# Four more inner tiles of the output weights by seven block products, and the tail woven from token halves

## The chip, the cores and the metric

The kernel runs on one core of a Trainium2 chip (trn2). A core has TensorE (PE, matmuls into PSUM, which has eight banks of 512 floats per partition), VectorE (DVE), ScalarE (ACT), GpSimd (POOL) and SyncE (SP). Each engine works off its own list of instructions in order and waits on semaphores for the others. DMAs are issued here from SP's and POOL's lists, and a few from ScalarE's. The metric is device time in microseconds, the median of several runs; lower is better.

## The reference

One decoder block on 512 tokens of width 1024: a SwiGLU feed-forward (FFN1), a token-mixing layer (pooling and dilated attention), a second SwiGLU (FFN2), each behind an RMSNorm that the conditioning vector scales and shifts, and a final RMSNorm.

```python
D_MODEL, SEQ, D_FF = 1024, 512, 2816
def swiglu(u, w_in, w_out):
    a, b = jnp.split(u @ w_in, 2, axis=-1)
    return (jax.nn.silu(a) * b) @ w_out

u = modulate(rmsnorm(h, g_norm_ffn1[l]), sh1, sc1)
h = h + 0.5 * gt1 * swiglu(u, w_ffn1_in[l], w_ffn1_out[l])
u = modulate(rmsnorm(h, g_norm_mix[l]), sh2, sc2)
h = h + gt2 * token_mixing(u, ...)
u = modulate(rmsnorm(h, g_norm_ffn2[l]), sh3, sc3)
h = h + 0.5 * gt3 * swiglu(u, w_ffn2_in[l], w_ffn2_out[l])
return rmsnorm(h, g_final)
```

The change is in the two products with w_out, [512 x 2816] by [2816 x 1024].

## The kernel before

**Layout and precision.** Activations lie transposed: a tile is 128 features by 512 tokens. The inner width 2816 is 22 inner tiles (`FT`), the output width 1024 is eight output tiles `H[0..7]` (`KT`), which hold the residual stream. Each float32 operand is split in a high and a low part of type fp32r, and a product is three matmuls: high by high, high by low, low by high (`mm3`, lines 358 to 360). ScalarE makes the high part of a weight chunk (`split_hi`, line 313), VectorE the low part (`split_lo`, line 327).

**Chunks.** `plan` lists in `order` all weight chunks in the order in which matmuls take them, and in `loads` the DMAs from HBM (512 KB a chunk of 1024 columns). Loads go to five buffers: three `raw` ones, and two parts of `X` in the FFNs. The split parts go into a ring of seven chunks (`RING`). `look(n)` issues loads into free buffers and splits chunks up to n ahead of the one that is taken next; `take` hands over the next one. `shift` and `shifted` only move where in the ring a chunk begins, by 16 columns.

**Seven products.** A product of two by two blocks needs eight block products; a scheme of sums and differences needs seven (Strassen's, in Winograd's form). For the weights, `blocks` lays a group of four loads out as seven chunks, of which four are differences that `make` computes on VectorE (line 252). A chunk listed in `outer` gets its low part in another way: ScalarE writes its negated high part (line 309) and POOL issues a DMA that adds the chunk from HBM (line 311). Token halves T1 and T2 (256 columns each) are the blocks of the other side. `duo` does two inner tiles of the first product of an FFN that way (lines 769 to 771), and `out_quad` four inner tiles of the second (lines 891 to 893), into three pairs of PSUM banks A, B, C, with partial sums copied to SBUF (`D`, line 873). `h_sums` makes the sums of the inner activations that it needs (lines 853 to 859), and `later` and `step` put such work a number of products later.

**Order of an FFN.** `ffn` goes through `PARTS` of the inner tiles. For each part it computes the inner tiles that are due (`ffn_pair` plain, or `duo`), and then that part's share of the output: plain matmuls for the first part of FFN1, `out_quad` for other parts, and for the last part, tiles 16 to 21, a **tail**: eight chunks of 768 columns, the first ones by 512 columns (lines 1053 to 1056), the last four or five output tiles by token halves (`out_tail` for FFN1, `out_end` for FFN2), a bank to each tile and half.

**End of an FFN.** For each tile VectorE updates H (`scalar_tensor_tensor`, line 515), ScalarE squares it (line 516), VectorE adds the squares up (`acc`). `stats_t` brings the sum over features by tiny matmuls (line 449), a square root on ScalarE and a reciprocal on VectorE (line 454); `spread` spreads the result over partitions by two matmuls (line 459). The first token half's statistics are taken while matmuls of the second half run. After FFN1 `norm_steps` computes the mixing stage's operands UH and UL from it (lines 466, 478, 492) and `head` begins that stage, with the splits of its first four chunks made ahead. After FFN2 `out_end` scales the tiles (line 567), multiplies by the spread reciprocal (line 571, VectorE and POOL) and stores them (line 574).

**Looking ahead.** Inside `out_quad` and later duos five chunks ahead are split; in the first duo of each FFN `look(3 + i // 3 if first else 5)`; `ffn_pair` three or four. The first `out_quad` is at 145 us (FFN1) and 722 us (FFN2) of the profile.

Of the kernel before, what the change touches and what calls it, by code (L numbers as in the profile page):

```python
# [14 lines left out]
P = 128  # L15
T = 512
# [39 lines left out]
def lay_ffn(w_in, w_out, first, plain, blocks):  # L56
# [16 lines left out]
    for k0, k1 in PARTS:  # L73
        if blocks <= k0 and k1 < FT:
            for i, c in ((0, 0), (0, 4), (1, 4), (1, 0)):
                rows = w_out[(k0 + 2 * i) * P:(k0 + 2 * i + 2) * P]
                quads.append(np.concatenate([_fmajor(rows, x) for x in _tiles(*((c + m) * P for m in range(4)))], axis=1))
            continue
        for m in range(KT):
            outs.append(_fmajor(w_out[k0 * P:k1 * P], np.arange(m * P, (m + 1) * P)))  # L80
    n = len(outs) - KT
    outs = [np.concatenate(outs[i:i + 2], axis=1) for i in range(0, n, 2)] + outs[n:]
    return ins, outs[:-KT] + quads + outs[-KT:]
# [43 lines left out]
PARTS = ((0, 4), (4, 8), (8, 12), (12, 16), (16, 22))  # L127
# [8 lines left out]
def chunk_widths():  # L136
    outs = [D] * (KT // 2 * (len(PARTS) - 1)) + [(FT - PARTS[-1][0]) * P] * KT
# [5 lines left out]
class Kernel:  # L143
# [6 lines left out]
    def plan(self):  # L150
# [12 lines left out]
        self.shifted, self.outer = set(), {}  # L163
# [8 lines left out]
        def blocks(recs, outer=0):  # L172
# [5 lines left out]
            self.shifted.update(range(len(self.order), len(self.order) + 7))  # L178
# [14 lines left out]
        def ffn(n, ins, outs, first):  # L193
# [4 lines left out]
            for part, (k0, k1) in enumerate(PARTS):  # L198
                while j < pairs_before(n, part):
# [8 lines left out]
                put = blocks if (n or part) and part < len(PARTS) - 1 else plain  # L208
                put(outs[part * KT // 2:(part + 1) * KT // 2] if part + 1 < len(PARTS) else outs[-KT:],
                    **({"outer": (3, 0, 2)[n]} if put is blocks else {}))  # L210

        ffn(0, f1i, f1o, FIRST)
        shift(3)
# [5 lines left out]
        shift(4)  # L219
# [298 lines left out]
    def out_tail(self, ms, ksrc, gate, nxt, squares):  # L518
# [5 lines left out]
        step = None  # L524
# [32 lines left out]
    def out_end(self, ms, ksrc, gate):  # L557
# [3 lines left out]
        tiles = {}  # L561
        A, Bh = slice(0, HT), slice(HT, T)
        rA, rB = self.B[6], self.B[7]
        self.held = self.pos

        def scaled(m, hs):
            nc.scalar.activation(self.O[m][:, hs], self.H[m][:, hs], AF.Copy, scale=self.g(3)[:, m:m + 1])

        def final(e, m, hs, r):
            o = self.O[m][:, hs]  # L570
            e.tensor_tensor(o, o, r[:, hs], op=OP.mult)

        def store(m0, m1, hs, queue):
            queue.dma_start(self.out[m0 * P:m1 * P, hs].rearrange("(m p) t -> p m t", p=P), self.OO[:, m0:m1, hs])

        for h, hs in enumerate((A, Bh)):
            for m in ms:
                bank = self.nb()
                if h == 0:
                    tiles[m] = ksrc(m)  # L580
                    self.split_hi()
                    if m == ms[0]:
                        nc.scalar.preload_act_table(AF.Sqrt)
                n = len(tiles[m])
                for i, (hi, lo, uh, ul) in enumerate(tiles[m]):
                    if h and m == ms[1] and i == n // 2:
                        self.stats_t(rA, A)
                    if h and m == ms[2] and i == n // 2:
                        self.spread(rA, A)
                        nc.scalar.activation(self.R[:, A], rA[:, A], AF.Copy)  # L590
                        for j in range(4):
                            final(g, j, A, self.R)
                            if j % 2:
                                store(j - 1, j + 1, A, nc.sync)
                    self.mm3(bank[:, hs], hi, lo, uh[:, hs], ul[:, hs], i == 0, i == n - 1)
                s = self.tp.tile([P, T], F32, name="ut")[:, :HT]
                self.tail_step(m, hs, bank, gate, s)
                if h and m == ms[-1]:
                    break
                scaled(m, hs)  # L600
                self.split_lo()
                v.tensor_tensor(self.acc[:, hs], self.acc[:, hs], s, op=OP.add)
                if h and m in ms[2:4]:
                    j = 4 + 2 * (m - ms[2])
                    for x in (j, j + 1):
                        final(v, x, A, rA)
                    store(j, j + 2, A, nc.sync)

# [7 lines left out]
        self.stats_t(rB, Bh, (self.acc[:, Bh], s))  # L616
        warm(2)
        scaled(ms[-1], Bh)
# [16 lines left out]
    def head(self, n, banks, table):  # L635
# [9 lines left out]
        for h, hs in enumerate((A, Bh)):  # L645
            for i, (k, which) in enumerate(steps if h == 0 else [(k, both) for k in range(KT)]):
                if h == 0:
                    stepA(min(i, 5) + 3)
                    if i == 4:
                        self.stats_t(self.B[7], Bh)  # L650
# [34 lines left out]
    def hpair(self, j):  # L685

        if self.nh == 4 and j == PARTS[-1][0] + 4:
            if not self.extra:
                self.extra = self.fw.tile([P, 2 * T], F32R, name="kept2"), self.Gall[:, :2 * T]
            return self.extra  # L690
# [19 lines left out]
    def ffn_pair(self, j, beside=lambda: None):  # L710
# [4 lines left out]
        pb = self.ffn_tile(ahead)  # L715
# [57 lines left out]
    def duo(self, j, first, last):  # L773
# [19 lines left out]
        HHp, HLp = (q(x) for x in self.hpair(j))  # L793
# [5 lines left out]
        def high():  # L799
            copy(HHp[:, :, ts, :], q(c)[:, :, ts, :])  # L800
# [927 lines left out]
```

## Time and profile before

| | us |
|---|---|
| median of 3 runs | 1002.2 (1002.18 to 1004.14) |
| the profiled execution, its own time | 1001.14 |
| its span, first to last instruction | 999.4 |
| TensorE busy | 984.8 |
| VectorE busy | 807.2 |
| ScalarE busy | 544.9 |
| tail of FFN1, first matmul to the mixing stage's first | 319.06 to 353.20 |
| tail of FFN2, first to last of its matmuls | 954.41 to 988.66 |

A row of the profile's groups names line, engine, operation, output and inputs with shapes and count, then busy time and the mean of one in ns, then idle time ahead of it and what ended it. Rows of the timeline begin with start and duration in us. A matmul's duration holds its way through the array, so matmuls overlap; from start to start they are closer than the duration says.

### The profile page before, as it was taken

To read this page: it belongs to the slowest core of one execution; us is meant where nothing else is said; L and a number is where in the kernel's file an instruction comes from. 1 tells how busy PE (TensorE), PEld (TensorE's weight loads), DVE (VectorE), ACT (ScalarE), POOL (GpSimd) and SP (SyncE) were. 2 spreads that over 40 slices of the span, in tenths; PEclk is the share of its full clock that TensorE was granted. 3 is DMA by queue.
4 is the path that set the end of the run, shared out by engine and by line. 5 is a ranking of instruction groups with operands and counts; after the bars stand their busy time and mean duration, and the time that the engine had idled before them with its cause. 6 is when DMAs were issued, how large, how long until landed. Compare 5 with 4: busy or idle time off the path is not lost.

```text
span 999.4 us, 17017 instructions
## 1 busy us (share of the span) xinstructions
PE 984.8 (99%) x6868; PEld 915.4 (92%) x6868; DVE 807.2 (81%) x1229; ACT 544.9 (55%) x824; POOL 67.0 (7%) x75
## 2 busy tenths in 40 slices
PE   8999999999999999999999999999999999999997
PEld 6888899999999999889988888898999999999996
DVE  6979979999996677879567777569798989989654
ACT  6453277786766443333414233465577868676652
POOL 0000001110110000007100000000010110010001
PEclk9999999999999999999999999999999999999999
DMA  9867567867857223123265774323376567567502
GB/s 338 278 212 251 190 169 211 222 184 216 241 126 198 89 78 106 57 92 125 77 235 185 266 267 133 96 73 106 111 169 192 143 171 179 156 151 204 137 17 85
DMA packets 49601, 163.29 MB, mean 163 GB/s; under 512 B 5617, under 2 KB 8945, under 8 KB 49522
## 3 DMA queue, kind: packets, MB, share of 16 engines
q1 hardware_dynamic: 42354, 137.95, 40.5%
q0 software_dynamic: 6480, 23.60, 14.2%
q8 instruction: 54, 0.88, 0.4%
q10 hardware_dynamic: 688, 0.66, 0.2%
q14 instruction: 25, 0.20, 0.1%
HBM read 159.41 MB, written 2.77 MB: 162 GB/s over the span
## 4 chain that ended last, share of the span: by engine, by line
PE 94%; DVE 3%; DMA 1%; ACT 1%; issue 1%; DVEq 0%; ACTq 0%; POOLq 0%
PE bank L358 13%; PE bank L359 13%; PE bank L360 13%; PE bank L771 10%; PE bank L769 10%; PE bank L770 10%; PE bank L891 4%; PE bank L893 4%; PE bank L892 4%; PE bank L1658 2%; PE bank L1662 1%; PE bank L1660 1%; PE bank L1249 1%; DMA wlo<-wf1o 1%; PE bank L1430 1%; PE bank L1431 1%
## 5 line engine op out<-in xcount | busy, mean ns | idle before, releaser
L327 DVE TENSOR_TENSOR wlo<-raw,whi 128x1024 fp32r<-128x1024 f32 (+5 forms) x129 | 140.3, 1099 | 45.3 <-ACT whi L313 45.1
L313 ACT ACTIVATE whi<-raw 128x1024 fp32r<-128x1024 f32 (+5 forms) x157 | 148.1, 955 | 18.9 <-DMA raw<-wmix 6.3
L358 PE MATMUL bank<-UH,whi 128*128 128x512 f32 (+1 forms) x432 | 158.1, 366 | 0.0
L359 PE MATMUL bank<-UL,whi 128*128 128x512 f32 (+1 forms) x432 | 154.0, 357 | 0.1
L360 PE MATMUL bank<-UH,wlo 128*128 128x512 f32 (+1 forms) x432 | 153.9, 356 | 0.0
L771 PE MATMUL bank<-UH,wlo 128*128 128x256 f32 x512 | 141.4, 276 | 0.0
L769 PE MATMUL bank<-UH,whi 128*128 128x256 f32 x512 | 141.4, 276 | 0.0
L770 PE MATMUL bank<-UL,whi 128*128 128x256 f32 x512 | 141.4, 276 | 0.0
L769 PE MATMUL bank<-SH,whi 128*128 128x256 f32 x384 | 107.0, 279 | 0.0
L771 PE MATMUL bank<-SH,wlo 128*128 128x256 f32 x384 | 106.9, 278 | 0.0
L770 PE MATMUL bank<-SL,whi 128*128 128x256 f32 x384 | 106.8, 278 | 0.0
L313 ACT ACTIVATE whi<-X 128x1024 fp32r<-128x1024 f32 (+3 forms) x109 | 90.5, 854 | 20.8 <-DVE X L252 20.7
L770 PEld LDWEIGHTS bank<-UL,whi 128*128 128x128 f32 x512 | 96.2, 188 | 0.1
L769 PEld LDWEIGHTS bank<-UH,whi 128*128 128x128 f32 x512 | 96.1, 188 | 0.1
L327 DVE TENSOR_TENSOR wlo<-X,whi 128x1024 fp32r<-128x1024 f32 (+3 forms) x92 | 83.1, 927 | 16.1 <-ACT whi L313 16.0
L771 PEld LDWEIGHTS bank<-UH,wlo 128*128 128x128 f32 x512 | 96.1, 188 | 0.0
L360 PEld LDWEIGHTS bank<-UH,wlo 128*128 128x128 f32 x432 | 81.1, 188 | 12.1
L359 PEld LDWEIGHTS bank<-UL,whi 128*128 128x128 f32 x432 | 81.2, 188 | 11.8 <-issue 0.5
L358 PEld LDWEIGHTS bank<-UH,whi 128*128 128x128 f32 x432 | 81.2, 188 | 11.3 <-issue 0.5
L770 PEld LDWEIGHTS bank<-SL,whi 128*128 128x128 f32 x384 | 72.5, 189 | 0.0
L769 PEld LDWEIGHTS bank<-SH,whi 128*128 128x128 f32 x384 | 72.5, 189 | 0.0
L771 PEld LDWEIGHTS bank<-SH,wlo 128*128 128x128 f32 x384 | 72.4, 189 | 0.0
(340 smaller groups left out, 2402.5 us busy)
## 6 DMA issues: line engine op xcount, KB each, us to landing
ada<-wada SPq DMA_DIRECT2D x47, 512.0 KB, 5.3
raw<-wmix SPq DMA_DIRECT2D x43, 512.0 KB, 4.1
raw<-wf1i SPq DMA_DIRECT2D x32, 512.0 KB, 6.2
raw<-wf2i SPq DMA_DIRECT2D x30, 512.0 KB, 4.5
AR<-wada SPq DMA_DIRECT2D x16, 512.0 KB, 4.1
wlo<-wf2i POOLq DMA_DIRECT2D x16, 512.0 KB, 5.7
X<-wf2i SPq DMA_DIRECT2D x14, 512.0 KB, 5.2
raw<-wf1o SPq DMA_DIRECT2D x12, 512.0 KB, 5.0
```

Source lines behind the costliest of these rows:

```text
L313: self.nc.scalar.activation(self.hi[:, y], r[:, x], AF.Copy)
L327: self.nc.vector.tensor_tensor(self.lo[:, y], r[:, x], self.hi[:, y], op=OP.subtract)
L358: M(ps, hi, uh, start=start, stop=False)
L359: M(ps, hi, ul, start=False, stop=False)
L360: M(ps, lo, uh, start=False, stop=stop)
L769: M(o, hi, uh, start=start and p == 0 and k == 0, stop=False, skip_group_check=True)
L770: M(o, hi, ul, start=False, stop=False, skip_group_check=True)
L771: M(o, lo, uh, start=False, stop=k == 3, skip_group_check=True)
L891: M(o, hi, uh, start=start and m % 2 == 0 and k == 0, stop=False, skip_group_check=True)
L892: M(o, hi, ul, start=False, stop=False, skip_group_check=True)
L893: M(o, lo, uh, start=False, stop=k == 1, skip_group_check=True)
L1658: M(b, hi, self.UH[k], start=k == 0, stop=False)
```

## The change

The output weights' last part is split in two: tiles 16 to 19 go through `out_quad` like the parts ahead, and tiles 20 and 21 go plain, by token halves, in the new `out_last`, which takes the place of the sixth step's rest, of the seventh product and of the old tails. In the plan, two plain chunks of 1024 columns (`rest`) stand ahead of the last chunk of that group of seven. `out_tail`'s place in FFN1 and the loops of `out_end` go; `out_end` keeps what comes after the last matmul. `duo` and the last plain tile look five chunks ahead throughout, and the last duo's high and low parts come by `later` in any case. In FFN1 tiles 20 and 21 get buffers of their own (HX, HY), and the steps of `trig` that stand beside duos begin one duo earlier.

```diff
-PARTS = ((0, 4), (4, 8), (8, 12), (12, 16), (16, 22))
+PARTS = ((0, 4), (4, 8), (8, 12), (12, 16), (16, 20), (20, 22))
...
-    outs = [D] * (KT // 2 * (len(PARTS) - 1)) + [(FT - PARTS[-1][0]) * P] * KT
+    outs = [D] * (KT // 2 * (len(PARTS) - 1) + 2)
...
-        def blocks(recs, outer=0):
+        def blocks(recs, outer=0, rest=()):
...
+                if rest and make == (x0, r21, x1):
+                    self.tail.append(len(self.order))
+                    plain(rest)
...
+                if n or part:
+                    blocks(recs, (3, 0, 2)[n], outs[-2:] if part + 2 == len(PARTS) else ())
...
-        pb = self.ffn_tile(ahead)
+        pb = self.ffn_tile(ahead + (j + 1 == PLAIN[0]))
...
-            self.look(3 + i // 3 if first else 5)
+            self.look(5)
...
-        if last:
-            mult()
-            high()
-            low()
-        else:
-            self.later(1, mult)
-            n = 8 if self.nh == 4 and j % 4 == 0 else 2
-            self.later(n, high)
-            self.later(n, low)
+        self.later(1, mult)
+        n = 8 if self.nh == 4 and j % 4 == 0 and j < PARTS[-1][0] else 2
+        self.later(n, high)
+        self.later(n, low)
...
-        self.ffn_post(3, self.ffn_silu(3, pa), self.ffn_tile(4), lambda low: self.later(1, low))
+        self.ffn_post(3, self.ffn_silu(3, pa), self.ffn_tile(5), lambda low: self.later(1, low))
...
+                if tail:
+                    return tail(A, B, C, D, lambda m, w: product(bank, u, start, (m,), w))
...
+    def out_last(self, n, gate, A, B, C, D, product):
+        self.held = self.pos
+        w = self.take() + self.take()
+        h = [self.hh(k) for k in range(*PARTS[-1])]
...
+        def plain(banks, m, t, start=False):
+            for k in range(2):
+                (hi, lo), (hh, hl) = w[2 * m + k], h[k]
+                o = half(banks, m)
+                M(o, hi, hh[:, t], start=start and m % 2 == 0 and k == 0, stop=False, skip_group_check=True)
+                M(o, hi, hl[:, t], start=False, stop=False, skip_group_check=True)
+                M(o, lo, hh[:, t], start=False, stop=k == 1, skip_group_check=True)
...
+        def two(m, t, acc, first):
+            o = acc if first else sq[:, m % 4 // 2 * T:m % 4 // 2 * T + T]
+            for i in range(2):
+                square(m + i, t, o[:, i * HT:(i + 1) * HT])
+            for i in range(2):
+                scaled(m + i, t)
+            if not first:
+                v.tensor_tensor(acc, acc, o, op=OP.add)
...
+        for m in range(4):
+            plain(C, m, T1)
+            to_h(m, half(C, m), T1)
+            if m % 2:
+                two(m - 1, T1, self.acc, m == 1)
+        for b in range(2):
+            more()
+            for i in range(2):
+                plain(B, 4 + 2 * b + i, T1)
+            v.tensor_tensor(D[b][:, :, 0, :], r(B[b]), D[b][:, :, 0, :], op=OP.add)
+            for i in range(2):
+                to_h(4 + 2 * b + i, D[b][:, i, 0, :], T1)
+            two(4 + 2 * b, T1, self.acc, False)
+            self.split_lo()
+        w6 = self.take()
+        for b in range(2):
+            more()
+            for i in range(2):
+                plain(C, 4 + 2 * b + i, T2, True)
+            v.tensor_tensor(D[b][:, :, 1, :], r(C[b]), D[b][:, :, 1, :], op=OP.add)
+            for i in range(2):
+                to_h(4 + 2 * b + i, D[b][:, i, 1, :], T2)
+            two(4 + 2 * b, T2, late, b == 0)
+            self.split_lo()
+        step = None
+        for m in range(4):
+            more()
+            if m == 1:
+                self.stats_t(rA, T1, (self.acc[:, :HT], self.acc[:, HT:]))
+            elif m == 2:
+                self.spread(rA, T1)
+                if n:
+                    self.final_first(rA)
+                else:
+                    step = self.norm_steps(1, T1)
+                    step(0)
+            product(m, w6)
+            plain(A, m, T2)
+            s = sq[:, m * HT:(m + 1) * HT]
+            to_h(m, half(A, m), T2)
+            square(m, T2, s)
+            if m < 3:
+                scaled(m, T2)
+            if step:
+                step(1 if m < 3 else 3)
+            self.split_lo()
+            x = late[:, m % 2 * HT:m % 2 * HT + HT]
+            if m < 3 or not n:
+                v.tensor_tensor(x, x, s, op=OP.add)
+            self.fetch()
+            if n and m == 2:
+                self.final_second(rA)
```

Here `half(banks, m)` is one half of a bank: tiles 0 and 1 share a bank, tiles 2 and 3 the next. `to_h` is the update of H on VectorE, `square` and `scaled` are ScalarE's, `more` makes the high part of the next weight chunk if the mixing stage's four are not yet split. `final_first` has POOL multiply and SP store four tiles of the first token half, `final_second` has VectorE do the other four.

More of the change, by code (lines that the diff above doesn't have):

```diff
@@ L559, in out_end, with final_second @@
+    def final_second(self, rA):
+        nc, A = self.nc, slice(0, HT)
+        for j in range(4, KT):
+            self.final(nc.vector, j, A, rA)
+            if j % 2:
+                self.store(j - 1, j + 1, A, nc.sync)
+    def out_end(self, gate, parts):
         nc = self.nc
         v, g = nc.vector, nc.gpsimd
[L561 to L607, printed above, removed]
@@ L771, in product, with duo @@
                 M(o, lo, uh, start=False, stop=k == 3, skip_group_check=True)
-    def duo(self, j, first, last):
+    def duo(self, j, first):
         nc, v = self.nc, self.nc.vector
@@ L883, in out_quad, with product @@
         p5 = [r(p5[:, i * T:(i + 1) * T]) for i in range(2)]
-        def product(banks, u, start):
-            w = self.take()
-            for m in range(4):
+        def product(banks, u, start, ms=range(4), w=None):
+            w = w or self.take()
+            for m in ms:
                 o = banks[m // 2][:, m % 2 * HT:m % 2 * HT + HT]
@@ L914, in out_quad @@
                     copy(D[b][:, :, 0, :], r(A[b]))
-                elif i == 3:
+                elif i == 3 and not tail:
                     for m in (2 * b, 2 * b + 1):
@@ L919, in out_quad @@
                     copy(D[b][:, :, 1, :], r(A[b]))
-                elif i == 5:
+                elif i == 5 and not tail:
                     v.tensor_tensor(D[b][:, :, 0, :], r(B[b]), D[b][:, :, 0, :], op=OP.add)
@@ L996, in ffn @@
                 else:
-                    if not tail and j == k1:
+                    if j == k1:
                         self.h_sums(k0, PLAIN[n])
-                    self.duo(j, last, tail and j + 2 == FT)
+                    self.duo(j, last)
                     last = None
@@ L1003, in ffn @@
                 last = self.beside_out(part) or last
+            if part + 2 == len(PARTS):
+                self.sums.close()
+                if n:
+                    op = self.f2.enter_context(self.tc.tile_pool(name="f2o", bufs=1))
+                    self.OO = op.tile([P, KT * T], F32, name="out").rearrange("p (m t) -> p m t", m=KT)
+                    self.O = [self.OO[:, m, :] for m in range(KT)]
+                else:
+                    self.sums = ExitStack()
+                    xp = self.sums.enter_context(self.tc.tile_pool(name="f1x", bufs=1))
+                    self.extra = [xp.tile([P, 2 * T], F32R, name=x) for x in ("HX", "HY")]
+                nc.scalar.preload_act_table(AF.Sqrt)
+                self.out_quad(k0, gate, lambda *x: self.out_last(n, gate, *x))
+                continue
```

167 lines of the change are left out of this document (83 added, 84 removed).

## The prediction

> **What bounds the kernel now.** I read the page first, then TensorE's waits, then the stretches of the two tails, then single rows.
>
> ```profile
> span 999.4 us, 17017 instructions
> ...
> PE 984.8 (99%) x6868; PEld 915.4 (92%) x6868; DVE 807.2 (81%) x1229; ACT 544.9 (55%) x824; POOL 67.0 (7%) x75
> ```
>
> TensorE is busy for all but 14.6 us, so time goes where matmuls go, or where TensorE is made to wait. The waits, largest first inside the two FFNs (engine and line, what it waited for, us, times, longest):
>
> ```profile
> PE bank L893 <- DMA wlo<-wf1o: 1.3, 1, 1.3
> PE bank L891 <- ACT bank L873: 1.2, 1, 1.2
> PE bank L891 <- ACT sl L794: 0.7, 1, 0.7
> ```
>
> Stretches (us, then busy time and instructions of PE, PEld, DVE, ACT, POOL, then clock and DMA). First an output block by seven products without a wait, then the first such block of each FFN; then the old tail of FFN1 in full-width and half-token matmuls, then that of FFN2:
>
> ```profile
> 782.09:801.13 19.04, 19.04 (x170) 19.04 (x169) 17.69 (x23) 16.02 (x22) 2.17 (x3) 1.00 0.68 172
> 145.16:165.78 20.62, 19.33 (x171) 19.13 (x169) 19.40 (x25) 16.70 (x24) 1.75 (x2) 1.00 0.70 167
> 722.11:743.69 21.58, 19.65 (x170) 19.25 (x169) 20.39 (x27) 17.02 (x25) 2.67 (x3) 1.00 0.65 154
> ...
> 319.06:335.40 16.34, 16.34 (x74) 13.52 (x73) 10.88 (x12) 8.71 (x12) 0.00 (x0) 1.00 0.56 159
> 335.40:353.20 17.80, 17.80 (x154) 17.79 (x152) 11.34 (x24) 6.89 (x14) 0.00 (x0) 1.00 0.28 85
> ...
> 954.41:966.68 12.27, 12.27 (x57) 10.14 (x55) 7.21 (x8) 6.36 (x9) 0.00 (x0) 1.00 0.00 1
> 966.68:988.66 21.98, 21.98 (x189) 21.98 (x188) 10.80 (x25) 10.53 (x23) 3.01 (x4) 1.00 0.06 19
> ```
>
> The reader is to see three things. A block of 168 matmuls of 256 columns takes 19.04 us, **0.1133 each**; 72 of 512 columns take 16.34, 0.227 each: time goes by columns. The first block of FFN1 takes 20.62 and that of FFN2 21.58, so 1.6 and 2.5 us of waiting stand there. And both tails run without a wait, with VectorE at 50 to 65%: they have slack on VectorE, and TensorE sets them.
>
> **The change: matmuls.** The old tail has 6 weight tiles x 8 output tiles x 3 matmuls of 512 columns, which is 288 halves. The new one has 7 products of 24 halves (168) and 2 tiles x 8 x 2 halves x 3 (96): 264. So 24 fewer per FFN, 2.7 us, 5.4 in all, if nothing waits.
>
> **Weights and queues.** Six loads of 512 KB replace eight of 384 KB per FFN, the same bytes, and two issues fewer on SP. Three low halves in FFN1 and two in FFN2 now come by an accumulating DMA on POOL's queue, re-reading 512 KB each, with a negating copy on ScalarE. Four block differences on VectorE, the sums of the activations and wider splits come too. I cost these at nothing up to the sixth product: the block at 782.09 carries the same work (DVE 17.69 of 19.04, ACT 16.02) and does not wait. With that cover gone each VectorE operation of 1024 would cost its 1.2 us. The last duo's high and low halves, once immediate, are late in no case, since the first products do not read tiles 20 and 21.
>
> **Five chunks ahead.** In the first duo a chunk is split one product (2.7 us) earlier. What that meets:
>
> ```profile
> 137.30 9.49 DMA wlo<-wf1o
> ...
> 146.84 0.38 PE bank L893
> ```
> ```profile
> 702.98 0.69 DVE L670 TENSOR_TENSOR X<-u,bank 128x512 f32<-128x512 f32 x1 [1.16 <-PE bank L360]
> 704.37 0.69 DVE L680 TENSOR_TENSOR HK<-X,HI 128x512 fp32r<-128x512 f32 x1 [0.70 <-ACT HI L679]
> 707.45 1.23 DVE L736 TENSOR_TENSOR UL<-X,UH 128x1024 fp32r<-128x1024 f32 x1 [2.39 <-ACT UH L733]
> ```
>
> The DMA issued at 137.30 lands 1.6 us after its block began at 145.16; issued a product earlier it is there in time. In FFN2 VectorE idles 1.16, 0.70 and 2.39 us ahead of the stretch in which it is full; two splits moved there take about 2.4 us of work out of it. I take both waits away: 1.6 and 2.3, **-3.8 us**, bounds -3.8 and 0.
>
> **The new tail.** Here lies the doubt. After the sixth product all is one hand-written order: output tiles 0 to 3 of the first token half, pairs 4-5 and 6-7 of that half, the pairs of the second half, then tiles 0 to 3 of the second half, with the statistics of the first half ahead of tile 1 and their spreading ahead of tile 2. VectorE takes them in just that order. Rows for its operations (busy, mean ns) and for how one follows another:
>
> ```profile
> L515 DVE SCALAR_TENSOR_TENSOR H<-bank,mod,H 128x256 f32<-128x256 f32 x10 | 4.8, 482 | 4.6 <-PE bank L360 4.5
> ...
> L921 DVE TENSOR_TENSOR X<-bank,X 128x512 f32<-128x512 f32 x1 | 0.7, 692 | 0.4 <-PE bank L893 0.4
> ```
> ```profile
> L516 ACT ACTIVATE ut<-H 128x256 f32<-128x256 f32 x10 | 4.2, 418 | 11.5 <-DVE H L515 11.5
> ```
> ```profile
> 350.72 0.86 DVE L466 SCALAR_TENSOR_TENSOR ut<-H,mod,bank 128x256 f32<-128x256 f32 x2
> ```
> ```profile
> 979.35 0.28 PE L360 MATMUL bank<-HI,wlo 128*128 128x256 f32 x1
> ...
> 979.67 0.48 DVE L515 SCALAR_TENSOR_TENSOR H<-bank,mod,H 128x256 f32<-128x256 f32 x1 [0.70 <-PE bank L360]
> ```
> ```profile
> 985.81 0.87 DVE L602 TENSOR_TENSOR AR<-AR,ut 128x256 f32<-128x256 f32 x1 [0.55 <-ACT ut L516]
> ...
> 987.26 0.47 DVE L515 SCALAR_TENSOR_TENSOR H<-bank,mod,H 128x256 f32<-128x256 f32 x1
> ...
> 987.83 0.42 ACT L516 ACTIVATE ut<-H 128x256 f32<-128x256 f32 x1 [1.65 <-DVE H L515]
> ...
> 988.28 0.43 DVE L602 TENSOR_TENSOR AR<-AR,ut 128x256 f32<-128x256 f32 x1 [0.54 <-ACT ut L516]
> 988.62 0.75 DVE L571 TENSOR_TENSOR out<-out,bank 128x256 f32<-128x256 f32 x2
> ...
> 989.28 0.48 DVE L515 SCALAR_TENSOR_TENSOR H<-bank,mod,H 128x256 f32<-128x256 f32 x1
> ```
>
> An update of H takes 0.48 (0.39 where another follows: two such take 0.86), ScalarE's square starts 0.10 after it and takes 0.42, and the sum of squares starts 0.03 after that: VectorE stands idle in between. A **pair** in the new tail costs VectorE its block sum 0.69, two updates 0.39 + 0.48, 0.10 + 0.42 + 0.03 for the square, and the sum of 512 at 0.60 until the next: **2.7 us**. TensorE's matmuls of a pair take 12 x 0.1133 = **1.36**. VectorE becomes the bound.
>
> A wait that before has nowhere: tiles 0 and 1 lie in the two halves of one PSUM bank, and so do 2 and 3, and VectorE reads one half while TensorE's next tile is due in the other. Unhidden, this costs 0.73 each time (drain 0.16, 0.04 to the update, 0.48, and 0.05 back), at least 0. The nearest row is one where matmuls go to a bank that ScalarE is reading, the same bytes there:
>
> ```profile
> 729.97 0.39 PE L891 MATMUL bank<-ut,whi 128*128 128x256 f32 x1 [1.22 <-ACT bank L873]
> ```
>
> They waited 1.22 us for the read to end; I take it that they wait here too. [...]
>
> **FFN2, from the first plain matmul.** Tile 0 ends at 0.84, its update at 1.36; tile 1 runs from 1.41, update to 2.77; tiles 2 and 3 likewise, last update 4.38 to 4.86, square, sum until 6.1. Two pairs: 6.1 + 5.4 = 11.5. The pairs of the second half: the first has no sum, 1.5, the second 2.7: 15.7. Then tile 0's update, 15.7 to 16.2. TensorE: four tiles until 4.2, 48 matmuls until 9.6, tile 0 until 11.0, the statistics at 11.6 to 12.0, and then nothing until 16.2, when tile 1 may write. Tile 1 until 17.6, the spreading 0.44 (the row below, of the old tail), tile 2 until 19.6, update until 20.1, square and sum (0.87 beside POOL's products) until 21.4, four output products of 0.33 until 22.7, and only then tile 3's update. Up to there 144 halves, 16.3, and 22.7: 39.0 after the tail began. Before, 954.41 to 989.28: 34.9. From that update to the end the code is the same but for two tiny matmuls (0.1). **+4.2 us**. ScalarE's scaled copies fit in its gaps.
>
> ```profile
> 983.26 0.44 PE bank L459 x4
> ```
>
> **FFN1.** The same chain, with two splits of weights for the mixing stage in it (1.14 of VectorE each), one more and two block sums ahead of the first update (0.85): tile 0's update of the second half moves from 15.7 to 18.8, so TensorE stands from 12.2 to 19.4. Tile 1 until 20.7, spreading 21.2, tile 2 until 22.6. The next norm's operations go ahead of tile 2's update on VectorE:
>
> ```profile
> L466 DVE SCALAR_TENSOR_TENSOR ut<-H,mod,bank 128x256 f32<-128x256 f32 x9 | 4.2, 474 | 0.8 <-PE bank L459 0.8
> L492 DVE SCALAR_TENSOR_TENSOR UL<-ut,mod,UH 128x256 fp32r<-128x256 f32 x8 | 3.8, 481 | 0.4 <-ACT UH L478 0.4
> ```
>
> Tile 1's square and sum, two products, ScalarE's copy between, one difference: 23.8; the update until 24.3; tile 3 from there until 25.7, when the mixing stage's first matmul may start, its operands ready. 16.3 + 25.7 = 42.0; before, 319.06 to 353.20 = 34.1. **+7.9 us**.
>
> **The clock.** The granted clock is the third number from the end (1.00, then 0.55):
>
> ```profile
> 992.00:994.00 2.00, 0.41 (x4) 0.22 (x2) 1.10 (x4) 0.39 (x1) 0.63 (x1) 1.00 0.12 40
> 994.00:999.00 5.00, 0.00 (x0) 0.00 (x0) 1.07 (x4) 0.00 (x0) 0.78 (x2) 0.55 0.58 194
> ```
> ```profile
> 7.14 4.53 PE L1587 MATMUL bank<-H,ones 128*128 128x128 f32 x20
> ...
> 14.90 1.50 PE L1587 MATMUL bank<-H,ones 128*128 128x128 f32 x12
> ```
>
> With the matmuls over, the clock falls to half in the stretch after 994; and at the start the same matmul goes at 0.22 for some 4 us, later at 0.11. So a long wait may cost half speed for some 4 us after it: tiles 1 and 2 in FFN1 1.4 us each, of which some 1.8 in all reach the end, as VectorE's work runs on beside them; in FFN2 2.1 by the same count. The idle time at the end is some 2 us, after a sparse stretch; 7.2 us are well beyond it, 4.2 after dense work are near it. I take the loss in FFN1, **+1.8**, and not in FFN2; bounds 0 and 3.9. [...]
>
> **Sum:** -3.8 + 7.9 + 4.2 + 1.8 = +10.1. Against the profiled run's own 1001.1 (span 999.4 and 1.7 around it) that is 1011.2; the median of the runs is 1002.2, 1.1 higher, so **1012.3**.
>
> **Rivals.** (1) *TensorE stays the bound*: 2 x 2.7 fewer matmuls and the waits of 3.8 gone, 0.9 given back in FFN2, where four output products instead of two stand ahead of the last update: -8.3, **993.9**. One mechanism decides it: the pair's chain of 2.7 us. If the square's 0.55 and the sums hid beside other work, so that a pair fell to 1.4, TensorE would never wait. For it speaks VectorE's slack in the old tail, against it that no row shows a square and its sum nearer together. Chance 0.13. (2) *The chain binds, the banks don't*: without the bank waits the first loop ends 1.4 to 2.3 us earlier and the last two tiles don't wait; I get +2.8 for FFN2, +3.8 for FFN1, -3.8: 1005.0, and with part of the chain hidden too 1000.5 to 1004: chance 0.17, half of it within 0.2%. (3) *The first blocks still wait*, since loads and sums crowd them as before, or both clocks fall: up to 3.8 + 2.1 more, **1016 to 1018**: chance 0.1, beyond 1018.5 0.04.
>
> My forecast's chance is 0.6, its own range 1007 to 1016. With (2) and most of (3), 1002 to 1018.5 holds about 0.8. About 0.2%, 2 us, is what a measurement of this kernel can tell: below 1000.2 lies (1) and a little of (2), 0.14; within, 0.09; above, 0.77.
>
> **What would show it.** Right: TensorE's longest waits are new, in out_last, for the H update at tile 1 of the second half (4 us in FFN2, 7 in FFN1), and short ones of 0.7 at tiles 1 and 3 of the first; the waits of L893 and L891 in the first blocks are gone; the stretch after the sixth product takes over 20 us where its matmuls need 13.6. Wrong: that stretch takes 14 to 15 us, or VectorE is seen ahead of TensorE there.

## The result and the profile after

| | before | after |
|---|---|---|
| median of four runs, us | 1002.3 (1002.18 to 1004.14) | 1014.45 (1012.95 to 1015.43) |
| span of the profiled execution | 999.4 | 1011.7 |
| first `out_quad` of FFN1, first to next product | 20.62 | 19.04 |
| first `out_quad` of FFN2 | 21.58 | 19.04 |
| tail of FFN1, its first matmul to the mixing stage's first | 34.1 | 43.4 |
| tail of FFN2, its first matmul to the end of the last update of H | 35.4 | 41.0 |

The ratio is 1.0120, with a 95% interval of 1.0103 to 1.0138: the change makes the kernel 12 us slower. The span grew by 12.3. Laid side by side the two profiles give: first blocks -1.6 and -2.5, tail of FFN1 +9.3, tail of FFN2 +5.6, mixing stage +0.75 (its start to FFN2's first block, 368.9 and 369.7), and +0.84 ahead of FFN1's first block.

The head of the page of after:

```profile
span 1011.7 us, 17287 instructions
...
PE 987.1 (98%) x6962; PEld 921.9 (91%) x6962; DVE 830.9 (82%) x1264; ACT 567.5 (56%) x867; POOL 70.6 (7%) x80
```

TensorE is busy 2.3 us longer although 48 matmuls of 256 columns are gone, and 10 us more are idle. TensorE's waits of after, first in FFN1's tail after the sixth product, then in FFN2's (what waited, for what, us in total, times, longest):

```profile
PE bank L867 <- DVE H L931: 5.0, 2, 4.4
PE bank L925 <- DVE H L931: 1.7, 2, 1.1
PE bank L454 <- DVE AR L947: 1.5, 1, 1.5
...
PE bank L867 <- DVE H L931: 4.2, 2, 3.6
PE bank L925 <- DVE H L931: 1.2, 2, 0.6
```

L867 is a product's matmul in the second half, L925 a plain one in the first, L931 the update of H in `out_last`, L947 a sum of squares, L454 the statistics. All are waits for VectorE. Stretches of after, in the columns used before: the two first blocks; FFN1's six products, the rest of its tail, and two parts of that; then the same of FFN2:

```profile
146.00:165.04 19.04, 19.04 (x171) 19.04 (x169) 18.85 (x25) 16.05 (x24) 2.25 (x3) 1.00 0.64 171
731.39:750.43 19.04, 19.04 (x170) 19.04 (x169) 19.01 (x25) 16.43 (x23) 2.18 (x3) 1.00 0.68 168
...
318.32:334.64 16.32, 16.32 (x147) 16.32 (x145) 10.06 (x11) 13.85 (x19) 0.87 (x1) 1.00 0.63 177
334.64:361.73 27.09, 18.91 (x135) 18.04 (x134) 18.98 (x37) 9.56 (x21) 0.00 (x0) 0.81 0.16 59
348.60:353.90 5.30, 0.91 (x6) 0.82 (x6) 4.62 (x9) 1.66 (x5) 0.00 (x0) 0.50 0.27 100
353.90:358.80 4.90, 4.90 (x23) 4.90 (x24) 1.96 (x6) 1.07 (x4) 0.00 (x0) 0.50 0.00 0
...
961.15:977.47 16.32, 16.32 (x146) 16.32 (x145) 10.27 (x11) 11.91 (x17) 0.86 (x1) 1.00 0.29 53
977.47:1001.00 23.53, 18.05 (x135) 17.17 (x134) 14.02 (x30) 12.44 (x32) 2.36 (x4) 0.93 0.00 1
990.10:993.90 3.80, 0.23 (x3) 0.14 (x2) 3.20 (x7) 3.19 (x8) 0.00 (x0) 0.98 0.01 2
993.90:997.20 3.30, 3.27 (x15) 3.27 (x16) 0.89 (x3) 0.96 (x3) 0.00 (x0) 0.51 0.00 0
```

The reader is to see that up to the sixth product all goes as planned: 144 matmuls in 16.32 us, no wait, and full first blocks. The 96 plain matmuls and the last 24, 13.6 us of work, then take 27.1 and 23.5. In 348.60 to 353.90 and 990.10 to 993.90 TensorE stands, but for 0.9 and 0.2 us, while VectorE works, and behind each stretch the clock is at half: 23 matmuls in 4.90 us, 15 in 3.30. VectorE's timeline of FFN2 in after shows who is late:

```profile
990.65 0.68 DVE L972 TENSOR_TENSOR cond<-bank,cond 128x512 f32<-128x512 f32 x1
991.37 0.88 DVE L931 SCALAR_TENSOR_TENSOR H<-cond,mod,H 128x256 f32<-128x256 f32 x2
992.79 0.69 DVE L947 TENSOR_TENSOR u<-u,sl 128x512 f32<-128x512 f32 x1 [0.54 <-ACT sl L934]
993.40 0.48 DVE L931 SCALAR_TENSOR_TENSOR H<-bank,mod,H 128x256 f32<-128x256 f32 x1
994.36 0.43 DVE L1001 TENSOR_TENSOR u<-u,sl 128x256 f32<-128x256 f32 x1 [0.48 <-ACT sl L934]
...
996.90 0.48 DVE L931 SCALAR_TENSOR_TENSOR H<-bank,mod,H 128x256 f32<-128x256 f32 x1 [1.83 <-PE bank L927]
...
1001.66 0.48 DVE L931 SCALAR_TENSOR_TENSOR H<-bank,mod,H 128x256 f32<-128x256 f32 x1
```

A pair runs from 990.65 to 993.40, 2.75 us, with 0.54 of it waiting for ScalarE's square. Only then comes tile 0's update of the second half (993.40), which holds the bank of tile 1; tile 1's matmuls start at 993.9, and VectorE in turn waits 1.83 us for them at half speed. The two engines wait for each other in turn.

### The profile page after: what moved, and what is told of

Read it like the earlier page. It is cut to its first block, busy times and chain, and to the rows that moved or that the text cites. A ratio compares the mean times of both kernels' runs of the same rounds, so it can differ in the third digit from the quotient of the medians.

```text
span 1011.7 us, 17287 instructions
## 1 busy us (share of the span) xinstructions
PE 987.1 (98%) x6962; PEld 921.9 (91%) x6962; DVE 830.9 (82%) x1264; ACT 567.5 (56%) x867; POOL 70.6 (7%) x80
## 4 chain that ended last, share of the span: by engine, by line
PE 90%; DVE 6%; ACT 1%; issue 1%; DMA 1%; SPq 0%; DVEq 0%; ACTq 0%
PE bank L363 11%; PE bank L364 10%; PE bank L365 10%; PE bank L752 10%; PE bank L750 10%; PE bank L751 10%; PE bank L867 6%; PE bank L869 6%; PE bank L868 6%; PE bank L1714 1%; PE bank L1718 1%; PE bank L1716 1%; PE bank L1305 1%; DVE wlo L332 1%; DVE H L931 1%
## 5 line engine op out<-in xcount | busy, mean ns | idle before, releaser
L332 DVE TENSOR_TENSOR wlo<-raw,whi 128x1024 fp32r<-128x1024 f32 (+6 forms) x126 | 138.0, 1105 | 46.4 <-ACT whi L318 46.2
L318 ACT ACTIVATE whi<-X 128x1024 fp32r<-128x1024 f32 (+2 forms) x98 | 92.1, 953 | 15.8 <-DVE X L257 15.7
L332 DVE TENSOR_TENSOR wlo<-X,whi 128x1024 fp32r<-128x1024 f32 (+2 forms) x79 | 82.3, 1056 | 13.3 <-ACT whi L318 13.3
L867 PE MATMUL bank<-HI,whi 128*128 128x256 f32 x288 | 81.1, 282 | 9.2 <-DVE H L931 9.2
L869 PE MATMUL bank<-HI,wlo 128*128 128x256 f32 x288 | 80.4, 279 | 0.0
L868 PE MATMUL bank<-HK,whi 128*128 128x256 f32 x288 | 80.4, 279 | 0.0
```

Source lines behind the costliest of these rows:

```text
L318: self.nc.scalar.activation(self.hi[:, y], r[:, x], AF.Copy)
L332: self.nc.vector.tensor_tensor(self.lo[:, y], r[:, x], self.hi[:, y], op=OP.subtract)
L867: M(o, hi, uh, start=start and m % 2 == 0 and k == 0, stop=False, skip_group_check=True)
L868: M(o, hi, ul, start=False, stop=False, skip_group_check=True)
L869: M(o, lo, uh, start=False, stop=k == 1, skip_group_check=True)
```

## The experiments

Each was timed beside the kernel before on one chip; a ratio is to that kernel, and differences between two kernels are differences of these ratios (0.001 is 1.0 us). Tails are measured in each profile as in the table above:

| run | ratio (95% interval) | tail FFN1 | tail FFN2 |
|---|---|---|---|
| before | 1 | 34.1 | 35.4 |
| the change | 1.0120 (1.0103 to 1.0138) | 43.4 | 41.0 |
| look_alone | 0.9946 (0.9932 to 0.9961) | as before | 35.4 |
| no_look | 1.0154 (1.0134 to 1.0173) | 43.4 | 42.3 |
| first_banks | 1.0085 (1.0070 to 1.0099) | 41.9 | 40.3 |
| late_sums | 1.0078 (1.0065 to 1.0091) | 41.3 | 39.4 |
| last_banks | 1.0088 (1.0075 to 1.0101) | 38.8 | 38.3 |
| warm | 1.0161 (1.0142 to 1.0181) | 46.8 | 42.2 |
| warm2 | 1.0094 (1.0080 to 1.0108) | 43.2 | 39.7 |
| all3 | 1.0005 (0.9995 to 1.0015) | 35.0 | 35.3 |
| full2 | 0.9958 (0.9944 to 0.9972) | 34.2 | 31.9 |
| full2w | 0.9978 (0.9965 to 0.9992) | 34.2 | 31.9 |
| full3 | 0.9983 (0.9974 to 0.9993) | 34.2 | 31.9 |
| look_again | 0.9956 (0.9944 to 0.9968) | as before | as before |

**The look-ahead, alone and taken away.** Put into the kernel before, and taken out of the changed one:

```diff
-        pb = self.ffn_tile(ahead)
+        pb = self.ffn_tile(ahead + (j + 1 == PLAIN[0]))
...
-            self.look(3 + i // 3 if first else 5)
+            self.look(5)
...
-        self.ffn_post(3, self.ffn_silu(3, pa), self.ffn_tile(4), lambda low: self.later(1, low))
+        self.ffn_post(3, self.ffn_silu(3, pa), self.ffn_tile(5), lambda low: self.later(1, low))
```

> The kernel before with the look-ahead alone: five chunks in the first duo, five at the last plain tile; the old tails stay. If the first blocks' waits were a matter of when a chunk is loaded and split, both go: 1.6 us in FFN1 and 2.5 us in FFN2, together -4.1, some 998.2 us. If they only move on to a later block, or their going in the changed kernel is owed to the new plan of the tail, nothing changes: 1002.3 us.

> The changed kernel with the old look-ahead in the first duo and at the last plain tile. If the look-ahead is what removed the first blocks' waits, they are back: 1.6 and 2.5 us more than the changed kernel, some 1018.6 us, with the new tails as they were (43.4 and 40.5 us). If the new plan removed them, 1014.5 us.

Both came out by the first theory: -5.4 us alone (interval -6.8 to -3.9, which holds the -4.1 expected), and 3.4 us more than the change when it is taken out. The tail of no_look in FFN2 is 1.3 longer besides; the clock stood at half for 6.83 us there, and in the change for 3.41:

```profile
999.03:1005.86 6.83, 5.73 (x27) 5.73 (x28) 2.54 (x6) 2.77 (x8) 1.02 (x2) 0.50 0.00 1
```

The two first blocks in look_alone, and TensorE's waits for loads and ScalarE in no_look:

```profile
145.82:165.70 19.88, 19.88 (x171) 19.85 (x169) 19.06 (x25) 16.39 (x24) 2.47 (x3) 1.00 0.69 166
722.38:741.42 19.04, 19.04 (x170) 19.04 (x169) 18.41 (x25) 16.49 (x23) 2.19 (x3) 1.00 0.68 168
```
```profile
PE bank L867 <- ACT bank L849: 1.2, 1, 1.2
PE bank L869 <- DMA wlo<-wf1o: 1.0, 1, 1.0
PE bank L867 <- ACT sl L774: 0.6, 1, 0.6
```

The waits of before are back in no_look, under new line numbers, and gone in look_alone. There FFN1's block still takes 19.88, though nothing waits in it. In look_again, a second run of the same kernel, it takes 19.04:

```profile
145.63:164.67 19.04, 19.04 (x170) 19.04 (x169) 18.85 (x25) 16.06 (x23) 2.25 (x3) 1.00 0.71 174
```

**The first four tiles by whole banks.**

```diff
-        for m in range(4):
-            plain(C, m, T1)
-            to_h(m, half(C, m), T1)
-            if m % 2:
-                two(m - 1, T1, self.acc, m == 1)
+        for m in (0, 2):
+            for i in range(2):
+                plain(C, m + i, T1)
+            for i in range(2):
+                to_h(m + i, half(C, m + i), T1)
+            two(m, T1, self.acc, m == 0)
```

> The changed kernel with the first four plain tiles taken by whole banks: tiles 0 and 1, then both updates, then 2 and 3. If TensorE's waits of 0.74 us at tiles 1 and 3 come from the shared bank, and the VectorE chain behind them sets the tail, they go and the chain starts 1.2 us earlier in each tail: -2.4, some 1012.0 us. If the chain has slack there, the waits go and the time stays at 1014.5 us. If the wait is not for the bank, the waits of 0.74 us stay too.

TensorE's waits in FFN1's tail are then:

```profile
PE bank L867 <- DVE H L931: 5.3, 2, 4.7
PE bank L454 <- DVE AR L947: 1.9, 1, 1.9
```

The waits of L925 are gone, and 3.5 us of time with them (1.0120 to 1.0085); by the profiles the two tails give 2.2 of it, where 2.4 was expected. So the waits were for the bank's other half, and lay on the path: tile 0's update of the second half starts 14.65 us after the first plain matmul of FFN2 and not 15.93. The long wait stays, since the chain behind it is as long.

**The sums of squares later.**

```diff
             if not first:
-                v.tensor_tensor(acc, acc, o, op=OP.add)
+                put.append(lambda: v.tensor_tensor(acc, acc, o, op=OP.add))
...
                 to_h(4 + 2 * b + i, D[b][:, i, 0, :], T1)
+            due()
             two(4 + 2 * b, T1, self.acc, False)
```

> The changed kernel with each sum of squares in out_last put behind the next pair's block sum and updates, so that VectorE does not stand idle for the square. By the chain of 2.7 us a pair, VectorE's idle 0.5 us a pair goes: tile 0's update of the second half comes 2.0 us earlier in each tail, and the shorter wait may spare the clock: -4 to -6, some 1009.5 us. If the bank waits or TensorE set the tail, 1014.5 us; and the statistics of the first half wait 0.5 us longer in any case.

-4.2 us (1.0120 to 1.0078). A pair of late_sums on VectorE, FFN2:

```profile
984.94 0.68 DVE L979 TENSOR_TENSOR X<-bank,X 128x512 f32<-128x512 f32 x1
985.66 0.88 DVE L931 SCALAR_TENSOR_TENSOR H<-X,mod,H 128x256 f32<-128x256 f32 x2
986.46 0.68 DVE L947 TENSOR_TENSOR AR<-AR,sl 128x512 f32<-128x512 f32 x1
987.06 0.68 DVE L979 TENSOR_TENSOR cond<-bank,cond 128x512 f32<-128x512 f32 x1
```

The pair takes 2.12 us from block sum to block sum, with no idle time in it. Tile 0's update comes 13.92 us after the first plain matmul in FFN2 (15.93 in the change) and 16.65 in FFN1 (18.72): 2.0 and 2.1, as expected.

**The last four tiles by whole banks.**

```diff
-            product(m, w6)
-            plain(A, m, T2)
+            for x in ((0, 1), (2, 3), (), ())[m]:
+                product(x, w6)
+                plain(A, x, T2)
```

> The changed kernel with the last four tiles of the second half taken by whole banks, 0 and 1 ahead of the statistics and 2 and 3 behind them, none behind the spreading; VectorE's order stays. By the shared bank, TensorE's waits of 3.8 and 4.7 us at tile 1 go, the reciprocal and the later updates no longer wait for matmuls: the last update comes 3.1 us earlier in FFN2, the mixing stage starts 3.5 us earlier in FFN1: some 1008 us. If VectorE's chain is as late without those waits, TensorE waits for it elsewhere, and the time stays within 1 us of 1014.5.

A miss in size: -3.2, where -6.5 was expected. FFN2's tail gave 2.7 of the 3.1, and the mixing stage did start 4.6 us earlier. But then last_banks takes 9.50 for the first stretch of that stage, where the change takes 6.74; the first line is last_banks, the second the change:

```profile
359.09:368.59 9.50, 9.50 (x60) 9.27 (x61) 7.29 (x19) 5.60 (x11) 0.00 (x0) 0.72 0.13 36
```
```profile
361.73:368.47 6.74, 6.74 (x62) 6.74 (x61) 5.31 (x14) 4.39 (x8) 0.00 (x0) 1.00 0.16 51
```

2.8 us are given back there, with the clock at 0.72. How much of it is the clock's stays open: the same stretch takes 8.6 us in full2w and full3 below, where the clock is full. And TensorE waits for VectorE elsewhere, in FFN1 ahead of the spreading, for the reciprocal:

```profile
PE bank L464 <- DVE r L459: 2.8, 1, 2.8
```

**Constant matmuls in the long wait.** The second run has 12 and 15 of them in place of 36 and 28:

```diff
+            for _ in range((15 if n else 12) if m == 1 else 0):
+                M(B[0][:, :P], self.ones, self.ones, start=True, stop=True)
             product(m, w6)
             plain(A, m, T2)
```

> The changed kernel with 36 (FFN1) and 28 (FFN2) matmuls of 128 columns on a constant, into a bank that is free, ahead of tile 1 of the second half: they fill most of TensorE's long wait and change no result. If the wait costs the clock and the slow matmuls lie on the path, the granted clock stays at 1.00 there and tile 1 ends 1.4 us earlier in FFN1 and 1.5 in FFN2: some 1011.5 us. If VectorE's chain alone sets the tail, the clock stays full and the time at 1014.5 us. If the clock falls for another reason, it still falls.

> The changed kernel with 12 (FFN1) and 15 (FFN2) constant matmuls ahead of tile 1 of the second half. Each takes two passes over the array, so in the run called warm 36 and 28 of them took 9.9 and some 6 us and outlasted the wait; these take 4.4 and 3.3 us and fit in it. If half speed after the wait lies on the path, tile 1 ends 1.4 us earlier in FFN1 and 1.5 in FFN2: some 1011.5 us. If VectorE alone sets the tail, the time stays at 1014.5 us.

warm was badly sized, and takes 4.1 us more than the change: each such matmul is two records, and FFN1's 36 outlast the wait. Its row, of TensorE's timeline:

```profile
347.77 9.91 PE L990 MATMUL bank<-ones 128*128 128x128 f32 x72
```

warm2 gains 2.6 us (1.0120 to 1.0094), about what was expected; its tails give 1.55 of it, 1.3 in FFN2 and 0.25 in FFN1. The stretches of warm2 behind the wait, FFN1 and FFN2:

```profile
353.00:356.00 3.00, 2.94 (x14) 2.94 (x15) 0.64 (x4) 0.57 (x2) 0.00 (x0) 0.55 0.01 4
...
993.00:996.00 3.00, 2.85 (x25) 2.76 (x25) 1.37 (x5) 1.52 (x5) 0.00 (x0) 1.00 0.00 0
```

In FFN2 the clock stays full, and tile 1 takes half as long: the price of the clock there is 1.3 us. In FFN1 the constant matmuls ended 1.96 us before tile 1 could start, and the clock fell all the same, so its price there is not measured by this run.

**All three edits together.**

> first_banks, last_banks and late_sums together. Followed through by the durations of the changed kernel's profile, the last update of FFN2 comes 18.8 us after the first plain matmul and not 24.7, and FFN1 gains about as much: -12, some 1002.5 us. If the wait of TensorE at the end then costs the clock in the mixing stage, up to 1005 us. If the three remove the same time, no better than the best of them alone, some 1008 us.

-11.5 us against the change, against -12 expected: 1.0005, the time of before. The edits, which gain 3.5, 4.2 and 3.2 alone, add up, since each takes another part of one chain. The clock fell here, too: all3 in the first 3.46 us of the mixing stage,

```profile
351.94:355.40 3.46, 3.46 (x15) 3.23 (x16) 3.46 (x9) 2.02 (x5) 0.00 (x0) 0.51 0.02 5
```

15 matmuls where 30 fit. What that costs stays open, since that stage's first stretch takes 8.63 us here and 8.57 in full2w, where the clock is full.

**Can the new tail beat the old one?** full2 has the edits of first_banks and late_sums and, in the last four tiles, this:

```diff
+        for b in range(2):
+            ms = (2 * b, 2 * b + 1)
+            for m in ms:
+                product(m, w6)
+                plain(A, m, T2)
+            if b:
+                self.spread(rA, T1)
+                if not n:
+                    step = self.norm_steps(1, T1)
+                    step(0)
+            for m in ms:
+                to_h(m, half(A, m), T2)
+            due()
+            if not b:
+                self.stats_t(rA, T1, (self.acc[:, :HT], self.acc[:, HT:]))
...
+        if n:
+            self.final_first(rA)
+            self.final_second(rA)
...
-            self.out_end(gate, (*self.late, s))
+            self.out_end(gate, (*self.late, s[:, :HT], s[:, HT:]))
```

> The three edits of all3, and the last four tiles written by banks on VectorE too: both updates of a bank one after the other, their sum of squares later by 512 or (for the last bank of FFN2) by the statistics' own matmuls, the first half's output products of FFN2 behind the last update, the next norm's first operations of FFN1 ahead of the last two updates. If VectorE's chain is what is left above TensorE's time, the last update of FFN2 comes 3.5 us earlier than in all3 and the mixing stage starts 1.6 us earlier, with no half-speed stretch behind it (2.1 us): -6 against all3, some 996 us, and below the kernel before with the look-ahead alone (997.7). If the end of FFN2 is set by other work (statistics, products, stores), only FFN1's part is seen: some 999 us.

> full2 with five constant matmuls (FFN1, 1.1 us) and eight (FFN2, 1.8 us) behind the first half's spreading, where TensorE would wait. If half speed follows in full2, these keep the clock at 1.00: up to 3 us less than full2 (2.1 in the mixing stage, 1.3 at the end). If the clock stays full in full2 anyway, no difference, or up to 1 us more where the matmuls outlast the wait.

> full2 with five constant matmuls behind the spreading in FFN1 alone, two instead of five ahead of the last statistics in FFN2, and in FFN1 the next norm's second tile ahead of the sum of squares. In the profile of full2w the last statistics wait 1.7 us behind constant matmuls while their operands are there: by that the end comes 1.7 us earlier than in full2w (span 996.9), and the mixing stage's start loses 0.7 us less: some 997 us, level with or below the kernel before with the look-ahead alone. If the output products and stores set the end instead, no change against full2w: 999.5 us.

> look_alone once more, on the same chip as full3, since the two are to be told apart by a few tenths of a per cent. If the new tail is worth its matmuls once nothing waits in it, full3 is 2 us or more below this one; if its saved matmuls only uncover VectorE's work behind them, the two agree within 2 us. This one should be at 0.9946 of the kernel before again.

All three beat the kernel before, by 1.7 to 4.2 us, and none beats the look-ahead alone: full2 (0.9958) is level with it (0.9946 and 0.9956), full3 is 2.7 us above look_again on the same chip, with intervals that do not touch. That is less than expected: full2 came to 999.2 where 996 was expected, full3 to 1000.3 where it was 997. The tails did what was asked: last updates of FFN2 3.4 us earlier than in all3. But from there to the end it takes 12.0 us in full3, 11.0 in all3 and 9.6 in the change; in full2 and full3 the first half's output products stand there. In full2 the clock fell in the mixing stage, and five constant matmuls in full2w held it; a stretch of either:

```profile
354.60:358.00 3.40, 3.40 (x18) 3.40 (x18) 3.40 (x10) 1.73 (x4) 0.00 (x0) 0.50 0.37 101
```
```profile
355.00:358.40 3.40, 3.40 (x32) 3.35 (x31) 3.40 (x10) 1.76 (x4) 0.00 (x0) 1.00 0.34 96
```

By the profiles that is worth 2.4 us in FFN1 (45.1 and 42.75 from the tail's start to the mixing stage's second stretch), but the medians of full2 and full2w, 999.2 and 999.9, do not show it; full2w's runs lie between 998.6 and 1003.6. Where the matmuls' gain went is seen in full3 and look_again, from the start of FFN1's tail to the same point of the mixing stage, and from the start of FFN2's tail to the end; first full3, then look_again:

```profile
317.92:360.67 42.75, 41.22 (x349) 39.83 (x347) 33.49 (x59) 27.21 (x48) 0.87 (x1) 1.00 0.42 115
953.97:997.90 43.93, 35.14 (x306) 34.53 (x304) 26.60 (x48) 25.41 (x53) 5.05 (x7) 0.91 0.26 69
```
```profile
317.95:358.59 40.64, 40.64 (x283) 37.68 (x281) 28.01 (x51) 19.95 (x34) 0.00 (x0) 1.00 0.39 112
951.00:995.90 44.90, 37.74 (x270) 35.14 (x268) 21.45 (x41) 18.34 (x36) 4.43 (x6) 0.93 0.14 48
```

The new tail needs 5.5 us more of VectorE in the first stretch and 5.2 in the second, for 2.7 us of matmuls each. FFN2 gains 1.0 by it, FFN1 loses 2.1. FFN1's tail itself is as long in both (34.2 and 34.1); the loss lies in the mixing stage's first stretch, 8.6 us in full3 and 6.5 in look_again. There three tiles in a row wait for the operand UL, of which VectorE makes one in 1.39 us. One of them, VectorE's row and TensorE's:

```profile
353.65 0.48 DVE L497 SCALAR_TENSOR_TENSOR UL<-ut,mod,UH 128x256 fp32r<-128x256 f32 x1
354.18 0.39 PE L364 MATMUL bank<-UL,whi 128*128 128x256 f32 x1 [0.25 <-DVE UL L497]
```

The rest of that stage takes 0.9 longer in full3. It is 362.4 to 362.7 us long in the three profiles with the old tail and 362.85 to 363.9 in the eleven with the new one; the cause stays open. A kernel with the old tail in FFN1 and full3's in FFN2 was not tried.

## Why the prediction was right, and where it was not

**Five chunks ahead, -3.8.** (The 1.6 and 2.3 given for it add up to 3.9.) Measured 1.58 + 2.54 = 4.1 in the profiles, and shown twice by runs: alone, and taken away. The span of possible values, -3.8 to 0, just missed it.

**Weights and queues, nothing.** Right: the six products take 16.32 us in both FFNs, without a wait.

**The chain of 2.7 us a pair.** Right, and shown by late_sums: with the 0.5 us idle for the square gone, a pair takes 2.1, and the tails shorten by 2.1 and 1.6. The calculation had tile 0's update of the second half at 15.7 us after the first plain matmul in FFN2 and 18.8 in FFN1; it came at 15.93 and 18.72.

**The shared banks, 0.73 a time.** Right: from start to start of the matmuls 0.74 is lost at tile 3 of FFN1 and at tiles 1 and 3 of FFN2 (0.6 each in the waits above, which count to the release alone). first_banks removes them and the time falls, which rules out the second rival. At tile 1 of FFN1 the wait is 1.1, since tile 0's update stands behind the two block sums.

**FFN1, one wait of 7 us.** The end was right (19.4 by the calculation, 19.25 measured for tile 1's start), the form was not: the statistics' matmuls stand ahead of tile 1, and they waited 1.5 us for VectorE's last sum of the first half, so the wait split into 1.5 and 4.4.

**The clock, "in FFN1 and not in FFN2".** This is the step that failed. It fell in both: in FFN2 for 3.4 us behind the wait of 3.6, in FFN1 for 10.2 us, from 348.6 on, which is behind the statistics' wait of 1.5 already. In FFN2 it cost 1.3 (warm2), and with it the term of +4.2 became +5.64; without it the tail would be 4.3 longer, which is the term as predicted. In FFN1 chain and clock together were put at 7.9 + 1.8 = 9.7 and came to 9.3; how the two share it stays open, since warm2 didn't hold the clock there, and with half speed for 10.2 us where some 4 were assumed the near hit is in part luck.

What stood ahead of the falls: in the change the stretch ahead of the one in FFN1, then for FFN2 from its sixth product's end to the wait, and the wait up to the fall; in warm2 four stretches of FFN1, in the last of which the clock falls; in full3 the two with the wait of 0.9 in FFN1 and behind it.

```profile
345.00:348.60 3.60, 2.07 (x19) 1.87 (x17) 3.02 (x6) 1.76 (x3) 0.00 (x0) 1.00 0.40 146
...
977.47:990.33 12.86, 11.56 (x94) 10.88 (x92) 8.05 (x16) 6.38 (x16) 0.00 (x0) 1.00 0.00 1
990.33:993.74 3.41, 0.00 (x0) 0.00 (x0) 2.83 (x7) 3.19 (x8) 0.00 (x0) 1.00 0.01 2
```
```profile
346.00:349.00 3.00, 1.74 (x15) 1.74 (x16) 2.45 (x5) 2.07 (x5) 0.00 (x0) 1.00 0.36 142
349.00:352.00 3.00, 2.10 (x19) 1.91 (x18) 2.42 (x5) 0.99 (x3) 0.00 (x0) 1.00 0.28 71
352.00:353.00 1.00, 0.00 (x0) 0.00 (x0) 1.00 (x2) 0.00 (x0) 0.00 (x0) 1.00 0.76 307
353.00:356.00 3.00, 2.94 (x14) 2.94 (x15) 0.64 (x4) 0.57 (x2) 0.00 (x0) 0.55 0.01 4
```
```profile
345.00:349.00 4.00, 3.13 (x27) 2.93 (x26) 3.96 (x8) 1.37 (x4) 0.00 (x0) 1.00 0.16 31
349.00:352.10 3.10, 2.97 (x25) 2.58 (x23) 2.11 (x7) 1.60 (x6) 0.00 (x0) 1.00 0.34 132
```

The prediction took 4.2 us after dense work for a case near the limit, and counted no loss. In FFN2 TensorE was busy for 11.56 of 12.86 us, then stood for 3.4, and the clock fell. In FFN1 it was busy for 2.07 of 3.60 us, and the clock fell all the same, 0.5 us after the statistics' wait of 1.53 had ended. In warm2, where 2.92 us of constant matmuls follow that wait, the clock stayed at 1.00 until 353 and fell behind the next one, of 1.96. No sharp limit is shown. By these cases the wait of some 4 us in FFN2 should have been priced as a likely loss, not as none.

**What wasn't in the sum:** +0.75 in the mixing stage and +0.84 ahead of the first block. The latter lies at the program's start, where profiled runs differ: the first block starts at 145.2 in before, 145.8 in look_alone, 144.5 in all3 and 148.0 in last_banks. Of the former 0.24 is the stage's first stretch (6.50 before, 6.74 after), and 0.5 lies in the rest of it, where the cause stays open. The sum of +10.1 stands against +12.3, and 1.3 of the gap is FFN2's clock.

**The rivals.** That TensorE stays the bound fell with the first profile. The later runs show more: even with TensorE's waits down to 0.9 and 0.7 us (full3) the 993.9 of that rival isn't reached, because VectorE's added work then stands ahead of the next stage, as the rows of full3 show. Of the third rival one half came true: both clocks fell, though at 1.3 and not 2.1 in FFN2, while the first blocks did not wait.

## What to carry to other kernels

Fewer matmuls at the end of a stage are worth something only if what follows each of them is no longer: here 2.7 us of TensorE cost 5 us of VectorE, right where the next stage waits for VectorE. Write out the order of a tail engine by engine, with the idle time between dependent operations; a pair's price of 2.7 and 1.36 us told before any run that VectorE would bind. A wait of TensorE of 1.5 us or more is to be priced with a chance of the clock's fall: here it fell behind 1.5, 1.96 and 3.6 us, and in FFN2 that cost 1.3. Give each PSUM bank's readers the whole bank at once (first_banks, -3.5 us), put a sum behind the next operations that don't need it (late_sums, -4.2), and test the parts of a change singly: here the part that looked least, the look-ahead, is the only one shown to make the whole kernel faster.

## What the runs showed of the hardware

- The clock fell to half behind short waits: in the change behind 1.53 us (FFN1's statistics), in warm2 behind 1.96 us. In full3, with 0.9 us of waiting there, it stayed full, and in warm2 it did so behind a wait of 1.53 as well, with 2.92 us of constant matmuls next: the length of a single wait does not tell alone.
- The same matmuls of 256 columns run 0.1133 us apart in one execution and 0.118 in another, without a wait in the views: FFN1's first block takes 19.88 in look_alone and 19.04 in look_again, which are the same kernel on two chips. So it isn't the code; no run here tells the cause.
- A constant float32 matmul of 128 by 128 columns is two records and not one in warm2, 0.12 us each: 24 records in 2.92 us for its 12.
